# Moving the next head's scores, finishes and fetches to earlier steps of the head loop, and the reloads of sent outputs one granule later

## The chip, the cores and the metric

The program runs on one core of one Trainium2 chip. The metric is the device time of one execution in microseconds (us). Three runs of the kernel before gave 2140.3, 2144.18 and 2147.97 us; the median is 2144.18 us.

## The reference

One transformer block: RMSNorm, native sparse attention with three branches (compressed, selected, sliding window) over 512 tokens and 16 heads, an output projection, RMSNorm, a SwiGLU feed-forward network and a final RMSNorm. All eight selectable key blocks are taken, so the selected branch attends to all earlier tokens, as the window branch does.

```python
hn = rmsnorm(x, mix_norm_g)
q, kc, vc, ks, vs, kw, vw, gl = split(hn @ w_in)     # 16 query heads, 4 key/value groups
gates = sigmoid(gl)                                   # three per head
s_c = q @ compress(kc).T + bias_c ; s_s = q @ ks.T + bias ; s_w = q @ kw.T + bias
o = gates[0] * softmax(s_c) @ compress(vc) + gates[1] * softmax(s_s) @ vs + gates[2] * softmax(s_w) @ vw
h = x + o @ w_out
out = rmsnorm(h + swiglu(rmsnorm(h, ffn_norm_g)), final_norm_g)
```

## The kernel before, in words

Nothing is scheduled by a compiler: each engine executes its instructions in the order in which the Python code emits them, and an instruction that has to wait holds everything behind it on its engine or queue. So the order of the calls in the source is the order on each of TensorE (PE), VectorE (DVE), ScalarE (ACT), GpSimd (POOL) and on the DMA queue of SyncE (SP).

Products are done in three matmuls of a split into a high and a low part (`three`, lines 266 to 269). A weight granule of 128 x 1024 numbers is loaded into `raw`, and split by one ACT copy (`whi`, line 97) and one DVE subtraction (`wlo`, line 98). In the attention phase the granules are loaded through POOL's queue. `W.take` splits two granules ahead of the one that is used, so at every start of a granule one `whi` and one `wlo` are emitted.

**The head loop** (lines 875 to 902) runs over 16 heads with 12 steps each. A step consists of calls for the current head h, of calls for the next head h + 1, and of `pump`, which lets a generator `dense()` emit a piece of dense work on PE.

- `scores(h+1, t)` for the query tiles t = 3, 2, 1, 0: PE computes the scores of 128 queries (`s`, one PSUM tile for all), DVE adds the bias and takes the maximum in three operations (line 797), and ACT takes three exponentials into `p` (line 799).
- `finish(h+1, t)`: DVE normalizes and gates `p` (lines 804 to 811), transposes it in 32 x 32 blocks (line 812), and SP writes it to `d_p[t]` in DRAM in four DMAs (line 814).
- `fetch(t)`: SP reads `d_p[t]` back with partitions rearranged into its place of the tile `PT` (`ptr` in the profile, line 818). It has to wait for the four writes, and for the last reader of its place.
- `turn(h, b, kt)`, called nine times in steps 0 to 8: ACT copies a part of `PT` to a high part (`pth`, line 835), DVE makes the low part (`ptl`, line 839; the ninth, line 837, in place). The first two read only the place of t = 3, the next two t = 2 and 3, and so on; the seventh and eighth, and the ninth, read all four.
- `values`: PE multiplies a turned part with the values into the PSUM tile `o`, two steps after its turn; the last at step 11, followed by `head_out` (line 855), which copies `o` out by ACT, for heads below 12 to `d_o` in DRAM.
- `load_bias(h + 2)` at step 4: a bias tile by SP.

In the order before, step by step (t in brackets): 0 fetch(1), turn, finish(h, 0); 1 turn; 2 turn, scores(3); 3 fetch(0), turn, finish(3); 4 and 5 turn, at 5 scores(2); 6 turn, finish(2); 7 turn; 8 turn, fetch(3), fetch(2), scores(1); 9 finish(1); 11 scores(0), last values, head_out. Ahead of the loop the same calls are made for head 0 (lines 868 to 874).

**The dense work** comes in 13 units of 20800 (a made-up time, 32 yields of 650), and then 4 of 15600. `pump` lets exactly one unit pass per head until `at` = 13: a unit ends with step 8. A unit has four granules of 8 yields, so a granule starts, and a weight split is emitted, in the `pump` of steps 0, 3 and 6; the fourth granule splits the first of the next unit in its middle (line 275), in step 7. Units are `qpair` (queries of two later heads), `kpair` and `vpair` (keys and values of the next group). Their results are evacuated by pairs: for a query, DVE scales it (`yt`, line 319), ACT makes the high part (`qh`, line 292), DVE the low part (`ql`, line 293), in the pumps of steps 7 and 8. `drain_to(needed(h+1))` forces the unit that the next head needs, if it isn't done.

The last unit with h0 = 14 uses the normalized input `hn` for the last time. As soon as its granules are used, `reload_o(i)` brings the outputs of four finished heads from `d_o[i]` to `hn_l` through POOL's queue (1 MB each, line 695), and `split_o(k)` splits those of two heads between `hn_h` and `hn_l` (lines 699 and 700). Then `partial(cb)` multiplies heads 0 to 11 with `w_out`, with the remaining `split_o` calls in its first unit.

Of the kernel before, what the change touches and what calls it, by code (L numbers as in the profile page):

```python
# [19 lines left out]
S, D, H, DH, G, HPG = 512, 2048, 16, 128, 4, 4  # L20
# [153 lines left out]
def nsa_block(ctx: ExitStack, tc: tile.TileContext, x, rel_bias, mix_g, ffn_g, fin_g, w_in, w_out,  # L174
# [96 lines left out]
    def ws(ps, gi, g, c0=0, c1=S, start=None, end=None, of=None):  # L271

        for u in range(2):
            cs = slice(128 * u, 128 * (u + 1))
            if end and gi == 3 and u:
                W.ahead(3)
            for k in range(4):
                kk = 4 * gi + k
                st = (kk == 0) if start is None else (start and kk == 0)
                three(ps[u][:, c0:c1], g[0][:, k, cs], g[1][:, k, cs],  # L280
                      *(x[:, kk, c0:c1] for x in of or (hn_h, hn_l)), st, kk == KC - 1)
                if end and gi == 3 and k == 3:
                    end(u)
                yield 650
# [57 lines left out]
    def q_out(ps, h0):  # L342
        def end(u):
            Q[h0 + u] = tuple(qp.tile([128, S], F32R, name=f"q{n}") for n in "hl")
            split_from(normed(ps[u], SCALE), Q[h0 + u][0], Q[h0 + u][1])

        return end
# [282 lines left out]
    with ExitStack() as st2:  # L630
# [18 lines left out]
        def proj2():  # L649
            pool_ = (psx, ps2)[next(units) % 2]  # L650
            return [pool_.tile([128, 512], F32, name="proj") for _ in range(2)]

        def qpair(h0):
            ps = proj2()
            end = q_out(ps, h0)
            for i in range(4):
                yield from ws(ps, i, W.take(), end=end)
                if h0 == H - 2 and i < 3:
                    reload_o(i)
                if h0 == H - 2 and i > 1:  # L660
                    split_o(i - 2)
            done["n"] += 1
            yield None

# [29 lines left out]
        def reload_o(i):  # L694
            pool.dma_start(hn_l[:, 4 * i:4 * i + 4].bitcast(F32), d_o[i].rearrange("h p s -> p h s"))

        def split_o(k):
            h, l = (x[:, 2 * k:2 * k + 2] for x in (hn_h, hn_l))
            act(h, l.bitcast(F32), AF.Copy)  # L699
            dve.tensor_tensor(l, l.bitcast(F32), h.bitcast(F32), op=OP.subtract)  # L700
# [41 lines left out]
        def pump(h, step):  # L742
            at = h + (step + 4) / STEPS
            goal = 20800 * min(at, 13) + 22500 * max(at - 13, 0)
            while done["ns"] < goal:
                c = next(stream, "end")
                if c == "end":
                    return
                done["ns"] += c or 0
# [8 lines left out]
        def needed(h):  # L758

            return 4 * ((h - 2) // 4) + (1 if h % 4 > 1 else 3) if h > 1 else 0  # L760
# [4 lines left out]
        def load_bias(h):  # L765
            if h < H:
                TB[h] = ap_.tile([128, S], F32, name="tb")
                (nc.sync if h else pool).dma_start(TB[h], bass.AP(tensor=d_u.tensor, offset=d_u.offset + h * UL + 127,
                                                 ap=[[H * UL - 1, 128], [1, S]]))
# [5 lines left out]
        def scores(h, t):  # L775
            g, n = h // HPG, 128 * (t + 1)
            (qh, ql), (kh, kl) = Q[h], KK[g % 2]
            if t == NT - 1:
                HS[h] = dict(
                    mx=ap_.tile([128, NT, 3], F32, name="mx"), sm=ap_.tile([128, NT, 3], F32, name="sm"))  # L780
            s = HS[h]
            at = 224 + (512 if t == 1 else 0)
            cuts = [0, 288] + [c for c in (800, 1056) if c <= 32 + 2 * n]
            if cuts[-1] < 32 + 2 * n:
                cuts.append(32 + 2 * n)
            for c0, c1 in zip(cuts, cuts[1:]):
                three(sc[:, at + c0:at + c1], qh[:, tok(t)], ql[:, tok(t)], kh[:, c0:c1], kl[:, c0:c1], True, True)
            c = CX[t][:, :NCMP]
            regions = [(c, c, c, sc[:, at:at + NCMP], biasc[:, h, 24 - 8 * t:24 - 8 * t + NCMP])]
            bt = TB[h][:, S - n:].rearrange("p (n s) -> p n s", s=128)  # L790
            sw = sc[:, at + 32:at + 32 + 2 * n].rearrange("p (n b s) -> p b n s", b=2, s=128)
            for b in range(2):
                u = ap_.tile([128, S], F32, name="u")[:, :n]
                regions.append((u.rearrange("p (n s) -> p n s", s=128), u.rearrange("p (n j s) -> p j n s", j=4, s=32),
                                branch(t, b).rearrange("p j (n s) -> p j n s", s=32), sw[:, b], bt))
            for i, (u, v, p, ps, bias) in enumerate(regions):
                dve.tensor_tensor_reduce(out=u, in0=ps, in1=bias, op0=OP.add, op1=OP.min, scale=-1.0,
                                         scalar=1e38, accum_out=s["mx"][:, t, i:i + 1])
                act(p, v, AF.Exp, bias=s["mx"][:, t, i:i + 1], scale=-1.0, accum_out=s["sm"][:, t, i:i + 1])
            s[t] = [c] + [branch(t, b) for b in range(2)]  # L800

        def finish(h, t):
            r = HS[h]["sm"][:, t]
            dve.reciprocal(r, r)
            dve.tensor_mul(r, r, gates[:, t, h])
            for i, p in enumerate(HS[h].pop(t)):
                o = p
                if not i:
                    o = P[t][:, :3, runs[t] - 32:]
                    p = CX[t].unsqueeze(1).to_broadcast([128, 3, 32])  # L810
                dve.tensor_scalar(o, p, r[:, i:i + 1], None, op0=OP.mult)
            dve.transpose(P[t], P[t])
            for i in range(4):
                nc.sync.dma_start(d_p[t][:, :, i].rearrange("j a r -> a j r"), P[t][32 * i:32 * (i + 1)])

        def fetch(t):

            nc.sync.dma_start(PT[:, :, PT_STEP * t:PT_STEP * t + runs[t]], d_p[t].rearrange("j a i r -> (j a) i r"))
# [6 lines left out]
        def turn(h, b, kt):  # L825
            n = S - 128 * kt
            th = ap_.tile([128, 512], F32R, name="pth", bufs=3)
            tl = ap_.tile([128, 512], F32R, name="ptl") if b >= 0 else th
            rows = 128 if b >= 0 else 96
            if b < 0:  # L830
                src = arrived(rows, 64, 0, PT_STEP + 64)
            else:
                src = arrived(rows, PT_STEP * kt + 32 * (kt + 1) * b + 32 * kt, kt, PT_STEP + 32 * b)
            th4, tl4 = (x[:rows, :n].rearrange("p (t i s) -> p t i s", i=4, s=32) for x in (th, tl))
            act(th4, src, AF.Copy)  # L835
            if b < 0:
                dve.tensor_tensor(th4[32:64], src[32:64], th4[32:64].bitcast(F32), op=OP.subtract)
            else:
                dve.tensor_tensor(tl4, src, th4.bitcast(F32), op=OP.subtract)  # L839
            HS[h]["t", b, kt] = th[:rows, :n], tl[:rows, :n]  # L840
# [27 lines left out]
        for i in range(4):  # L868
            scores(0, 3 - i)
            if i > 1:  # L870
                fetch(5 - i)
            if i:
                finish(0, 4 - i)
            pump(-1, min(9 + i, 11.7))
        for h in range(H):
            seq = [(b, kt) for kt in (3, 2, 1, 0) for b in (0, 1)] + [(-1, 0)]
            for i in range(STEPS):
                if i == 4:
                    load_bias(h + 2)
                if i in (0, 3):  # L880
                    fetch(1 - i // 3)
                if i < 9:
                    turn(h, *seq[i])
                if i == 8 and h + 1 < H:
                    fetch(3)
                    fetch(2)
                if i == 0:
                    finish(h, 0)
                if h + 1 < H:
                    if i == 2:  # L890
                        drain_to(needed(h + 1))
                    if i % 3 == 2:
                        scores(h + 1, 3 - i // 3)
                    elif i % 3 == 0 and i:
                        finish(h + 1, 4 - i // 3)
                if 2 <= i < 10 or i == 11:
                    if i == 2 and h % HPG == 0:
                        drain_to(h)
                    values(h, *seq[min(i - 2, 8)])
                    if i == 11:  # L900
                        head_out(h)
                pump(h, i)
# [592 lines left out]
```

## Time and profile before

| What | Value |
|---|---|
| median of 3 runs | 2144.18 us |
| the profiled execution, its own time | 2143.05 us |
| its span, first to last instruction | 2141.3 us |
| around the span | 1.75 us |
| mean granted TensorE clock | 0.993 |
| busy: PEld / DVE / ACT / POOL | 1951.4 / 1634.8 / 929.2 / 128.0 us |
| head loop | about 222 to 713 us |

The profile's views have these columns. A timeline row is start, duration, engine, line, operation, written tile <- read tiles, shapes, and in brackets the idle time ahead of it with the one who ended it; "x2" joins two neighbours. A waits row is engine, written tile and line <- releaser: total us, times, longest. A window row is the stretch, then the busy time (and instructions) of PE, PEld, DVE, ACT, POOL, the granted clock, the DMA share, and GB/s. Ends of matmuls are modelled and overlap, so a PE that is busy for a whole stretch may still wait a little.

### The profile page before, as it was taken

To read this page: it belongs to the slowest core of one execution; us is meant where nothing else is said; L and a number is where in the kernel's file an instruction comes from. 1 tells how busy PE (TensorE), PEld (TensorE's weight loads), DVE (VectorE), ACT (ScalarE), POOL (GpSimd) and SP (SyncE) were. 2 spreads that over 40 slices of the span, in tenths; PEclk is the share of its full clock that TensorE was granted. 3 is DMA by queue.
4 is the path that set the end of the run, shared out by engine and by line. 5 is a ranking of instruction groups with operands and counts; after the bars stand their busy time and mean duration, and the time that the engine had idled before them with its cause. 6 is when DMAs were issued, how large, how long until landed. Compare 5 with 4: busy or idle time off the path is not lost.

```text
span 2141.3 us, 37148 instructions
## 1 busy us (share of the span) xinstructions
PE 2105.8 (98%) x14697; PEld 1951.4 (91%) x14697; DVE 1634.8 (76%) x2674; ACT 929.2 (43%) x1439; POOL 128.0 (6%) x209
## 2 busy tenths in 40 slices
PE   9999999999979999999999999999999999999998
PEld 7898788898969889899999999999999888989996
DVE  5565777877767347898888888888888787877785
ACT  5344455555544234434434344344344444544344
POOL 1000111111101000000000000000000000001000
PEclk9999999999989999999999999999999999999999
DMA  7554666666757633344434344343443776878894
GB/s 232 179 148 147 186 197 197 183 197 188 217 179 233 221 127 128 109 137 130 127 120 126 122 129 129 119 128 119 129 128 126 253 277 217 295 272 309 307 331 151
DMA packets 271867, 388.08 MB, mean 181 GB/s; under 512 B 34523, under 2 KB 204555, under 8 KB 271052
## 3 DMA queue, kind: packets, MB, share of 16 engines
q1 hardware_dynamic: 245932, 275.52, 41.0%
q0 software_dynamic: 23856, 105.98, 14.2%
q10 hardware_dynamic: 1904, 4.20, 0.5%
q8 instruction: 115, 1.88, 0.4%
q14 instruction: 60, 0.49, 0.1%
HBM read 320.52 MB, written 70.36 MB: 183 GB/s over the span
## 4 chain that ended last, share of the span: by engine, by line
PE 67%; DMA 1%; DVE 1%; ACT 1%; issue 0%; SPq 0%; ACTq 0%; DVEq 0%
PE f L268 19%; PE f L269 19%; PE f L267 19%; PE proj L267 1%; PE proj L268 1%; PE proj L269 1%; PE pp L267 1%; PE pp L268 1%; PE pp L269 1%; PE po L268 1%; PE po L267 1%; PE po L269 1%; DMA tt<-d_a 0%; PE pp L245 0%; DMA d_p<-p 0%
## 5 line engine op out<-in xcount | busy, mean ns | idle before, releaser
L98 DVE TENSOR_TENSOR wlo<-raw,whi 128x1024 fp32r<-128x1024 f32 (+1 forms) x226 | 270.7, 1200 | 115.2 <-ACT whi L97 115.1
L97 ACT ACTIVATE whi<-raw 128x1024 fp32r<-128x1024 f32 (+1 forms) x226 | 234.4, 1040 | 223.2 <-DVE raw L994 121.7
L994 DVE TENSOR_TENSOR tlo<-tt,thi 128x1536 fp32r<-128x1536 f32 (+2 forms) x135 | 197.1, 1460 | 109.7 <-ACT thi L1096 88.8
L267 PE MATMUL f<-hn_h,whi 128*128 128x256 f32 x984 | 271.7, 276 | 0.8 <-ACT E L1054 0.8
L269 PE MATMUL f<-hn_h,wlo 128*128 128x256 f32 x984 | 271.6, 276 | 0.0
L268 PE MATMUL f<-hn_l,whi 128*128 128x256 f32 x984 | 271.6, 276 | 0.0
L1091 ACT ACTIVATE whi<-raw 128x1024 fp32r<-128x1024 f32 x123 | 126.1, 1057 | 292.2 <-DVE raw L994 282.0
L267 PE MATMUL proj<-hn_h,whi 128*128 128x512 f32 x512 | 205.4, 401 | 0.5 <-ACT hn_h L402 0.5
L268 PE MATMUL proj<-hn_l,whi 128*128 128x512 f32 x512 | 201.7, 394 | 0.3 <-DVE hn_l L403 0.3
L269 PE MATMUL proj<-hn_h,wlo 128*128 128x512 f32 x512 | 201.6, 394 | 0.0
L267 PEld LDWEIGHTS f<-hn_h,whi 128*128 128x128 f32 x984 | 184.7, 188 | 1.2 <-ACT E L1054 1.2
L269 PEld LDWEIGHTS f<-hn_h,wlo 128*128 128x128 f32 x984 | 184.7, 188 | 0.0
L268 PEld LDWEIGHTS f<-hn_l,whi 128*128 128x128 f32 x984 | 184.7, 188 | 0.0
L1096 ACT ACTIVATE thi<-tt 128x1536 fp32r<-128x1536 f32 x82 | 121.9, 1487 | 84.1 <-PE f L268 84.1
L267 PE MATMUL proj<-whi,hn_h 128*128 128x256 f32 (+2 forms) x496 | 146.6, 296 | 5.9 <-ACT hn_h L699 5.9
L269 PE MATMUL proj<-whi,hn_l 128*128 128x256 f32 (+2 forms) x496 | 146.0, 294 | 2.1 <-DVE hn_l L700 2.1
L994 DVE TENSOR_TENSOR wlo<-raw,whi 128x1024 fp32r<-128x1024 f32 x123 | 147.0, 1223 | 0.0
L268 PE MATMUL proj<-wlo,hn_h 128*128 128x256 f32 (+2 forms) x496 | 145.5, 293 | 0.0
L269 PE MATMUL f<-whi,tlo 128*128 128x512 f32 x320 | 124.9, 390 | 0.6 <-DVE tlo L994 0.6
L268 PE MATMUL f<-wlo,thi 128*128 128x512 f32 x320 | 125.0, 391 | 0.3 <-DVE wlo L98 0.3
L267 PE MATMUL f<-whi,thi 128*128 128x512 f32 x320 | 124.7, 390 | 0.0
L839 DVE TENSOR_TENSOR ptl<-ptr,pth 128x128 fp32r<-128x128 f32 (+3 forms) x128 | 60.0, 485 | 76.7 <-ACT pth L835 72.9
(327 smaller groups left out, 6142.6 us busy)
## 6 DMA issues: line engine op xcount, KB each, us to landing
raw<-in_ffn_w_in SPq DMA_DIRECT2D x135, 512.0 KB, 3.6
raw<-in_ffn_w_out SPq DMA_DIRECT2D x88, 512.0 KB, 5.9
rawx<-in_ffn_w_in SPq DMA_DIRECT2D x41, 512.0 KB, 4.9
rawx<-d_a SPq DMA_DIRECT2D x31, 512.0 KB, 4.9
ah<-d_s POOLq DMA_DIRECT2D x16, 896.0 KB, 7.4
al<-d_s POOLq DMA_DIRECT2D x16, 896.0 KB, 10.1
raw<-in_nsa_w_in SPq DMA_DIRECT2D x24, 512.0 KB, 4.6
raw<-in_nsa_w_in POOLq DMA_DIRECT2D x24, 512.0 KB, 4.4
```

The source lines that it names most:

```text
L97: self.nc.scalar.activation(hi[:, :n], src, AF.Copy)
L98: self.nc.vector.tensor_tensor(lo[:, :n], src, hi[:, :n].bitcast(F32), op=OP.subtract)
L267: mm(o, ah, bh, start=start, stop=False, skip_group_check=True)
L268: mm(o, ah, bl, start=False, stop=False, skip_group_check=True)
L269: mm(o, al, bh, start=False, stop=stop, skip_group_check=True)
L839: dve.tensor_tensor(tl4, src, th4.bitcast(F32), op=OP.subtract)
L994: dve.tensor_tensor(o, a, b, op=OP.subtract)
L1091: act(h, r, AF.Copy)
L1096: act(h, ttf, AF.Copy)
```

## The change

The head loop's calls for the next head move to other steps. In the new order: 0 fetch(0), turn, scores(3); 1 turn, finish(3); 2 turn; 3 turn, scores(2); 4 turn, finish(2); 5 turn; 6 turn, scores(1); 7 turn, finish(1); 8 turn, fetch(3), fetch(2); 9 fetch(1), scores(0); 10 finish(0); 11 last values, head_out. `pump`, `turn`, `values` and `load_bias` stay in their steps. In numbers of steps, scores and finishes come two steps sooner, fetch(1) and fetch(0) three.

```diff
@@ qpair
             for i in range(4):
                 yield from ws(ps, i, W.take(), end=end)
-                if h0 == H - 2 and i < 3:
-                    reload_o(i)
-                if h0 == H - 2 and i > 1:
-                    split_o(i - 2)
+                if h0 == H - 2 and i:
+                    reload_o(i - 1)
+                    if i == 3:
+                        split_o(0)
+                        split_o(1)
@@ the head loop
+        fetch(1)
+        finish(0, 0)
         for h in range(H):
             seq = [(b, kt) for kt in (3, 2, 1, 0) for b in (0, 1)] + [(-1, 0)]
             for i in range(STEPS):
+                more = h + 1 < H
                 if i == 4:
                     load_bias(h + 2)
-                if i in (0, 3):
-                    fetch(1 - i // 3)
+                if i == 0:
+                    fetch(0)
                 if i < 9:
                     turn(h, *seq[i])
-                if i == 8 and h + 1 < H:
+                if i == 8 and more:
                     fetch(3)
                     fetch(2)
-                if i == 0:
-                    finish(h, 0)
-                if h + 1 < H:
-                    if i == 2:
+                if i == 9 and more:
+                    fetch(1)
+                if more:
+                    if i == 0:
                         drain_to(needed(h + 1))
-                    if i % 3 == 2:
+                    if i % 3 == 0:
                         scores(h + 1, 3 - i // 3)
-                    elif i % 3 == 0 and i:
-                        finish(h + 1, 4 - i // 3)
+                    elif i % 3 == 1:
+                        finish(h + 1, 3 - i // 3)
```

## The prediction

> **What bounds the kernel now.** I read the busy times first, then stretches of one head each, then who waits for whom, and last the timeline of one head.
>
> ```profile
> PE 2105.8 (98%) x14697; PEld 1951.4 (91%) x14697; DVE 1634.8 (76%) x2674; ACT 929.2 (43%) x1439; POOL 128.0 (6%) x209
> ...
> 283.58:313.46 29.88, 29.88 (x185) 26.72 (x184) 23.49 (x65) 15.12 (x41) 4.48 (x6) 1.00 0.69 198
> 523.16:553.05 29.89, 29.89 (x185) 26.71 (x184) 23.48 (x65) 15.24 (x43) 4.47 (x6) 1.00 0.69 200
> ```
>
> PE is busy for 98% of the span and for all of a head (two heads are shown, cut at their head_out), so whatever moves other work looks free, and at most some 35 us could be won. But the periods are equal to 0.02 us although the heads carry different dense units. Something with a fixed rhythm may set them. So I asked who waits in the undisturbed heads (240 to 585 us):
>
> ```profile
> DVE ptl L839 <- ACT pth L835: 48.5, 34, 2.2
> DVE ql L293 <- ACT qh L292: 8.6, 12, 0.7
> ...
> ACT cx L799 <- DVE mx L797: 112.0, 46, 3.7
> ...
> ACT pth L835 <- DMA ptr<-d_p: 1.2, 3, 0.6
> ```
>
> In the whole answers for DVE and ACT no row names PE: DVE waits for ACT alone, ACT for DVE and, for 1.2 us, for a fetch. The two hand work to each other in a closed loop, one head after the other. Here is one turn of it, ACT and then DVE:
>
> ```profile
> 523.64 0.30 ACT L835 ACTIVATE pth<-ptr 128x128 fp32r<-128x128 f32 x1
> ...
> 529.61 0.19 ACT L799 ACTIVATION_READ_ACCUMULATOR p<-u,mx 128x1 f32 x1
> ...
> 537.24 0.62 ACT L835 ACTIVATE pth<-ptr 128x512 fp32r<-128x512 f32 x1
> ...
> 543.86 1.05 ACT L97 ACTIVATE whi<-raw 128x1024 fp32r<-128x1024 f32 x1
> ...
> 548.40 0.19 ACT L799 ACTIVATION_READ_ACCUMULATOR p<-u,mx 128x1 f32 x1
> ...
> 553.52 0.30 ACT L835 ACTIVATE pth<-ptr 128x128 fp32r<-128x128 f32 x1
> ```
>
> ```profile
> 523.97 0.29 DVE L839 TENSOR_TENSOR ptl<-ptr,pth 128x128 fp32r<-128x128 f32 x1 [1.51 <-ACT pth L835]
> ...
> 525.80 1.18 DVE L98 TENSOR_TENSOR wlo<-raw,whi 128x1024 fp32r<-128x1024 f32 x1
> ...
> 527.43 0.18 DVE L797 CUSTOM_DVE_ANT_0 cx<-s,biasc 128x31 f32<-128x31 f32 x1
> ...
> 528.77 0.08 DVE L797 DVE_READ_ACCUMULATOR2_ANT mx<- 128x1 f32 x1
> 530.13 0.42 DVE L839 TENSOR_TENSOR ptl<-ptr,pth 128x256 fp32r<-128x256 f32 x1 [1.28 <-ACT pth L835]
> ...
> 535.32 0.18 DVE L797 CUSTOM_DVE_ANT_0 cx<-s,biasc 128x31 f32<-128x31 f32 x1
> ...
> 536.38 0.08 DVE L797 DVE_READ_ACCUMULATOR2_ANT mx<- 128x1 f32 x1
> 537.88 0.69 DVE L839 TENSOR_TENSOR ptl<-ptr,pth 128x512 fp32r<-128x512 f32 x1 [1.42 <-ACT pth L835]
> ...
> 543.99 0.69 DVE L293 TENSOR_TENSOR ql<-yt,qh 128x512 fp32r<-128x512 f32 x1 [0.70 <-ACT qh L292]
> 544.94 1.23 DVE L98 TENSOR_TENSOR wlo<-raw,whi 128x1024 fp32r<-128x1024 f32 x1 [0.26 <-ACT whi L97]
> 546.20 0.68 DVE L837 TENSOR_TENSOR pth<-ptr,pth 32x512 fp32r<-32x512 f32 x1
> 546.91 0.19 DVE L797 CUSTOM_DVE_ANT_0 cx<-s,biasc 128x31 f32<-128x31 f32 x1
> ...
> 547.71 0.08 DVE L797 DVE_READ_ACCUMULATOR2_ANT mx<- 128x1 f32 x1
> ...
> 549.14 0.69 DVE L293 TENSOR_TENSOR ql<-yt,qh 128x512 fp32r<-128x512 f32 x1 [0.74 <-ACT qh L292]
> 549.75 0.17 DVE L804 RECIPROCAL sm<-sm 128x3 f32<-128x3 f32 x1
> ...
> 551.76 0.15 DVE L797 CUSTOM_DVE_ANT_0 cx<-s,biasc 128x31 f32<-128x31 f32 x1
> ```
>
> From the first turn to the next head's is 553.52 - 523.64 = 29.88 us. DVE's idle brackets in it sum to 1.51 + 1.28 + 1.42 + 0.70 + 0.26 + 0.74 = 5.91 us; busy 23.5 and some joints make the rest. So the loop of DVE and ACT is full, and as slow as PE. **Two engines bound the heads together**, and a longer loop is paid in full, head by head.
>
> **The change, part by part.**
>
> **Scores against weight splits.** Instructions and bytes stay the same; only the order changes. Before, the step after scores begins with a turn and a finish, so ACT makes `whi` while DVE works on the finish, and `wlo` (525.80) needn't wait. Now scores(3), scores(2), scores(1) stand in steps 0, 3, 6, right ahead of the pump that emits a split. Behind the score operations the next thing on DVE is `wlo`; on ACT the exponentials come first, then `whi`, and 1.08 us after its start (543.86 to 544.94) `wlo`. What I get for DVE's idle time behind each:
>
> - scores(3): DVE is through 1.34 us after its start (527.43 to 528.77); ACT's last read starts at 2.18 (529.61), so `whi` at 2.27, `wlo` at 3.35: idle 2.01 where it was 1.28.
> - scores(2): DVE through at 1.06, ACT free at 1.92 (537.24), `wlo` at 3.00: idle 1.94 for 1.42.
> - scores(1): DVE through at 0.80, ACT free at 1.58 (548.40 + 0.09), `wlo` at 2.66: idle 1.86. Before, queries' evacuation lay there, with 0.74; that wait stays, in step 8, at the 0.70 of its twin.
> - scores(0): finish(0) now waits for the exponentials alone, by the same rows some 0.9 us, and the turn that waited 1.51 no longer does.
>
> The sum is 2.01 + 1.94 + 1.86 + 0.70 + 0.26 + 0.70 + 0.9 = 8.4 us, 2.5 more than 5.91. A `wlo` that follows a wait also holds DVE for 1.26 us (544.94 to 546.20) and not 1.10: three times, at most 0.5. So the loop alone takes 32.4 to 32.9, I say 32.6 us. Queued behind the waiting `wlo` are the next `ptl` and finish, and PE's values wait for `ptl`. PE's work doesn't grow, but it cannot run on: it already stands within two steps of the turns.
>
> **Fetch(3) loses its lead.** It goes out when turn(8) has left the tile, and the next head's first turn needs it.
>
> ```profile
> ptr<-d_p SPq DMA_DIRECT2D x16, 576.0 KB, 5.7
> ...
> 576.43 1.22 SPq L818 DMA_DIRECT2D ptr<-d_p  x2
> ```
>
> Before, the DVE part of turn(8) starts 22.56 us after the first turn (546.20), ends 0.68 later, and the fetch lands at about 22.56 + 0.68 + 5.7 = 28.9, 0.9 us ahead of need. In the new order finish(0) leaves the stretch ahead of turn(8) (1.6 of the 1.83 us from 523.97 to 525.80), scores(1) (0.80) and finish(1) (549.75 to 551.76, 2.01) enter it, and the idle time in it grows from 3.66 to 2.01 + 1.94 + 1.86 + 0.96 = 6.77. Turn(8) then starts at 22.56 - 1.6 + 2.8 + 3.1 = 26.9, with the slower restarts up to 27.3; the fetch lands at 27.1 + 0.7 + 5.7 = 33.5. That is later than the loop's own 32.6. So **the head takes 33.5 us**, 3.6 more. Behind this fetch on SP stand fetch(2), fetch(1), the writes of finish(0) and `d_o`; they have several steps left.
>
> The Trainium skill (DMA: Bandwidth & Descriptors, Anatomy of one DMA) gives 2.0 us plus bytes at 436 GB/s, fitted for GpSimd's path. By that this fetch would take an estimated 3.4 us and be hidden, and the second rival below would hold; the trace's 5.7 is used.
>
> **How many heads.** Heads 1 to 11 pay 3.6 each: 39.6. Head 0 starts from the same fetch and pays the excess over its own old course, about 1. Early dips of PE stay as they are.
>
> **Head 12, reloads and outputs.** Here the old order loses time:
>
> ```profile
> 589.22 0.53 SPq L818 DMA_DIRECT2D ptr<-d_p  x1
> ...
> 596.96 0.94 ACT L835 ACTIVATE pth<-ptr 128x384 fp32r<-128x384 f32 x2 [6.22 <-DMA ptr<-d_p]
> 597.54 0.69 PE L267 MATMUL o<-pth,v1h 128*128 128x384 f32 x1 [2.62 <-ACT pth L835]
> ...
> 604.37 0.63 ACT L835 ACTIVATE pth<-ptr 128x512 fp32r<-128x512 f32 x1 [3.90 <-DMA ptr<-d_p]
> ...
> 611.04 0.50 PE L268 MATMUL o<-ptl,v1h 128*128 128x512 f32 x1 [1.97 <-DVE ptl L839]
> ...
> 618.39 0.58 PE L267 MATMUL proj<-whi,hn_h 128*128 128x256 f32 x1 [5.91 <-ACT hn_h L699]
> ...
> 621.28 0.58 PE L269 MATMUL proj<-whi,hn_l 128*128 128x256 f32 x1 [2.10 <-DVE hn_l L700]
> ...
> 630.34 0.50 ACT L835 ACTIVATE pth<-ptr 128x128 fp32r<-128x128 f32 x2
> ```
>
> Fetch(1) and fetch(0) go out beside the reloads, and ACT waits 6.22 and 3.90 us for them. Three steps sooner they land ahead of need; these 10.1 us go. What is late next is `split_o`: PE's first partial product now needs split_o(0) too, since three splits stand in a row behind scores(0). From the first turn (553.52 + 29.88 = 583.4) to the next head's (630.34) head 12 takes 47.0 us. New: queries done at 29.9, scores and exponentials to 31.2, first split on DVE at 32.3, three of about 1.2 to 35.8, finish(0) 1.6, a fourth split, head_out 0.7, a `wlo` and the next split: 41. So 6 us are won, less than the waits removed. Reload_o(2) now goes out beside fetch(3) of head 13. A fetch beside a reload cost ACT up to 6.22 us here; but in this head some 13 us lie between the fetch (27.6) and the next first turn (41), so I take 0, with 6 as the other end. Reload_o(0) no longer waits on POOL for PE; the load behind it waits for `wlo` anyway: 0. `drain_to` two steps sooner finds its unit done since step 8: 0.
>
> **Heads 13 to 15.** Splits there fall on other steps and PE has more work per head; I take 0 (-2 to +4). In the last head fetch(0) comes in time:
>
> ```profile
> 705.00:720.00 15.00, 13.27 (x66) 10.12 (x65) 7.14 (x10) 5.87 (x8) 1.47 (x2) 1.00 0.66 209
> ```
>
> The 1.73 us that PE lacks in this stretch go.
>
> **Sum** against the profiled execution's own 2143.05 (span 2141.3 and 1.75 around it): 1 + 39.6 - 6 - 1.7 = 32.9, so 2176. The median of the runs shown is 1.1 above that execution; I leave that aside.
>
> **Rivals.**
>
> - *The fetch stays hidden*: it lands in 4.6 us or less, or turn(8) comes sooner. Then the loop's 32.6 counts: 2.7 x 11 - 6 - 1.7 = +22, **2165**. For it: in the undisturbed heads a fetch was late only three times, by 1.2 us in all. Against: 0.9 us of lead, and 4.5 are taken away. Chance 0.23; it also is what the skill's figure leads to.
> - *The fetch is slower*: fetch(1) and a weight load now share the time, and ACT's wait for a fetch that went out at 589.22 ended 7.7 us later. At 7.5 us a head takes 35.3: 5.4 x 12 - 7.7 = +57, **2200**. Chance 0.10.
> - *The loop isn't the bound* and the change does what it is named for. If, behind the scores, ACT and DVE have slack that the brackets don't show, a head stays at 29.9 us or less, and only the old stalls go: 2.62 + 1.97 of head 12, half of the 8.0 behind it, 1.7 at the end: -10, **2133**. For it: PE is 100% busy in the heads, and the fetches come earlier. Against: DVE's brackets name ACT at every place. It decides from the first full head on: its period is above or below 29.9. Chance 0.14.
> - *Nothing to see* (within 0.3%, which is about what a measurement of this kernel can tell from no change): gain and loss cancel at 1.2 us more per head. Chance 0.03.
>
> **How the numbers follow.** The forecast has 0.50. With the slower cases that makes slower 0.83, same 0.03, faster 0.14. The likeliest case alone spans 2168 to 2187 (heads 13 to 15, and 0.5 us per head either way). The range takes in the hidden fetch and part of the slow one, and leaves out the gain: 2154 to 2195.
>
> **What would show it.** Period from head_out to head_out near 33.5 us and PE busy near 29.7 of it; brackets of 1.8 to 2.0 us at L98 naming `whi`, three per head; ACT waiting for `ptr` by 1 to 2 us at each first turn; no long `ptr` wait in head 12; a burst of three L699 there with PE idle for some 9 us ahead of them. A period below 30 us would make the prediction wrong; one of 32.6 without `ptr` waits, its second step.

## The result and the profile after

Four runs of the changed kernel gave 2173.24 to 2176.09 us, median 2174.78 us. Four runs of the kernel before, taken beside them, had a median of 2144.3 us. The ratio is 1.0142, with a 95% interval of 1.0123 to 1.0162: the change makes the kernel **slower by 1.4%**. The profiled execution took 2174.97 us with a span of 2173.2 us, 31.9 us more than the span before, at a clock of 0.995 (0.993 before). In the new kernel the lines behind the first edit are numbered one higher: the turn is L836, L838 (ninth) and L840, the scores L798 and L800, the fetch L819, the reload L696, `split_o` L700 and L701.

The page's busy times, and then two heads cut from first turn to first turn (stretch, length, busy PE, PEld, DVE, ACT, POOL, clock, DMA share, GB/s):

```profile
PE 2110.7 (97%) x14697; PEld 1947.0 (90%) x14697; DVE 1640.6 (75%) x2674; ACT 932.0 (43%) x1439; POOL 129.9 (6%) x209
```

```profile
253.09:286.25 33.16, 30.33 (x145) 24.61 (x144) 24.16 (x65) 15.58 (x43) 4.47 (x6) 1.00 0.60 166
554.70:588.01 33.31, 29.98 (x172) 25.69 (x171) 23.85 (x65) 15.34 (x40) 4.78 (x6) 1.00 0.59 167
```

No engine has more work to do: DVE's busy time grew by 5.8 us over the whole span, PE's by 4.9. A head takes some 33 us instead of 29.9, and now PE lacks 3 us in each of them at full clock. The share of PE in the span hardly moved (98% to 97%), which would be easy to read over.

Who waits, from 260 to 600 us (waiting instruction <- releaser: total us, times, longest), on DVE and then on ACT:

```profile
DVE wlo L98 <- ACT whi L97: 60.3, 41, 1.9
DVE ptl L840 <- ACT pth L836: 10.4, 10, 2.0
DVE ql L293 <- ACT qh L292: 7.0, 10, 0.7
DVE sm L805 <- ACT p L800: 6.6, 8, 0.8
```

```profile
ACT pth L836 <- DMA ptr<-d_p: 19.7, 10, 2.7
```

DVE's main wait has changed its name. Before, it was `ptl` on `pth`, 48.5 us; now it is the low part of a weight on its high part. And ACT waits for a fetch in every head (10 times in these 340 us). The timeline of one head shows both, on DVE (the first turn, the three weight splits behind scores, and the ninth turn) and on SP and ACT:

```profile
520.35 0.29 DVE L840 TENSOR_TENSOR ptl<-ptr,pth 128x128 fp32r<-128x128 f32 x1 [1.00 <-ACT pth L836]
...
523.90 1.23 DVE L98 TENSOR_TENSOR wlo<-raw,whi 128x1024 fp32r<-128x1024 f32 x1 [1.93 <-ACT whi L97]
...
531.86 1.23 DVE L98 TENSOR_TENSOR wlo<-raw,whi 128x1024 fp32r<-128x1024 f32 x1 [1.85 <-ACT whi L97]
...
539.56 1.22 DVE L98 TENSOR_TENSOR wlo<-raw,whi 128x1024 fp32r<-128x1024 f32 x1 [1.77 <-ACT whi L97]
...
547.16 0.68 DVE L838 TENSOR_TENSOR pth<-ptr,pth 32x512 fp32r<-32x512 f32 x1
```

```profile
547.87 3.01 SPq L819 DMA_DIRECT2D ptr<-d_p  x3
```

```profile
520.01 0.31 ACT L836 ACTIVATE pth<-ptr 128x128 fp32r<-128x128 f32 x1 [1.92 <-DMA ptr<-d_p]
...
554.70 0.31 ACT L836 ACTIVATE pth<-ptr 128x128 fp32r<-128x128 f32 x1 [2.69 <-DMA ptr<-d_p]
```

Read in order of time, this is the closed loop of the new kernel. Three times DVE stands nearly 2 us ahead of a `wlo`. The ninth turn comes 27.15 us after the first (547.16 - 520.01), the fetches go out when it has ended, and ACT, which has had nothing else to do for 2.69 us, starts the next head's first turn 6.83 us after the first of them was issued. This head, with 34.69 us, is the longest of the eleven; they run from 32.71 to 34.69 us, with a mean of 33.42.

Head 12 has one long gap of PE. It ends when the first of a burst of four `split_o` on ACT is done:

```profile
651.96 3.88 ACT L700 ACTIVATE hn_h<-hn_l 128x1024 fp32r<-128x1024 f32 x4
```

```profile
653.05 0.58 PE L267 MATMUL proj<-whi,hn_h 128*128 128x256 f32 x1 [10.05 <-ACT hn_h L700]
```

To compare kernels, I cut each at the start of its ninth turns on DVE (the 32 x 512 subtraction), which can be found in all of them. The numbers are us of one profiled execution each:

| kernel | to the first ninth turn | per head, 11 heads | heads 12 and 13 | last two heads | rest of the span |
|---|---|---|---|---|---|
| before | 246.84 | 29.90 | 76.17 | 59.91 | 1429.5 |
| after | 246.72 | 33.44 | 73.67 | 56.05 | 1429.0 |
| difference | -0.1 | +3.54 (11 heads: +38.9) | -2.5 | -3.9 | -0.5 |

So all of the loss is in the eleven full heads, and 7.0 us of it are won back elsewhere.

### The profile page after: what moved, and what is told of

It is laid out like the page before. It is cut to its first block, busy times and chain, and to the rows that moved or that the text cites. A ratio compares the mean times of both kernels' runs of the same rounds, so it can differ in the third digit from the quotient of the medians.

```text
span 2173.2 us, 37131 instructions
## 1 busy us (share of the span) xinstructions
PE 2110.7 (97%) x14697; PEld 1947.0 (90%) x14697; DVE 1640.6 (75%) x2674; ACT 932.0 (43%) x1439; POOL 129.9 (6%) x209
## 4 chain that ended last, share of the span: by engine, by line
PE 78%; DVE 9%; ACT 4%; DMA 4%; issue 4%; SPq 0%; DVEq 0%; ACTq 0%
PE f L269 18%; PE f L268 18%; PE f L267 18%; PE proj L267 5%; PE proj L268 5%; PE proj L269 5%; DMA ptr<-d_p 3%; ACT whi L97 2%; DVE p L812 2%; DVE ptl L840 2%; DVE wlo L98 2%; ACT p L800 1%; DMA d_p<-p 1%; PE pp L269 1%; PE pp L268 1%
## 5 line engine op out<-in xcount | busy, mean ns | idle before, releaser
L269 PEld LDWEIGHTS proj<-hn_h,wlo 128*128 128x128 f32 x512 | 96.4, 188 | 21.6 <-DVE wlo L98 0.2
```

What stands on the lines that cost most here:

```text
L269: mm(o, al, bh, start=False, stop=stop, skip_group_check=True)
```

## Experiments

The theory is that of the prediction: DVE and ACT form a full loop; weight splits right behind scores lengthen it to some 32.6 us, and the fetch of t = 3, which can't leave before the ninth turn, lifts that to 33.4. Against it stood: that the sooner scores and finishes cost by themselves, that only the fetch or only the splits count, and that PE sets the pace. Four kernels undo or redo one part of this; the next three part the two halves of the change; the last four ask where the floor is.

**The dense work one step later.** The changed kernel, with `pump` shifted by one step, so that splits no longer stand right behind scores:

```diff
-            at = h + (step + 4) / STEPS
+            at = h + (step + 3) / STEPS
```

> The changed kernel with the pump's clock one step later, so that weight splits fall on steps 1, 4 and 7, where the finishes stand, and a unit ends in step 9. Theory (the splits stood right behind the scores, and DVE idled through exponentials and whi): each finish covers whi again, the idle time in front of wlo goes from some 1.9 us, three times per head, to 0, the loop of DVE and ACT falls to 29.6 to 30 us, turn(8) comes some 5 us sooner and the fetch is hidden. Head 12 keeps what the earlier fetches won. So 2133 to 2138 us, faster than both kernels. Rival (the earlier scores or the fetch alone make the head long): the head stays at 32 us or more, 2160 to 2175 us.

Measured: 2131.24 us (2130.69 to 2132.03, 5 runs), ratio to the kernel before 0.9938 (0.9924 to 0.9952). The heads take 29.63 us. This is **faster than both kernels**, with every call of the change at its new step. DVE's and ACT's waits (260 to 570 us):

```profile
DVE ptl L840 <- ACT pth L836: 41.4, 34, 1.3
...
DVE wlo L98 <- ACT whi L97: 3.0, 10, 0.5
```

```profile
ACT pth L836 <- DMA ptr<-d_p: 1.6, 4, 0.9
```

The waits of `wlo` fall to 3.0 us, and with them the fetch comes in time: the ninth turn is soon enough again. What made the changed kernel slow was where the splits stood, not the sooner scores.

**The fetch taken out of the loop.** The changed kernel, with the first turn of a head put behind the scores of t = 3 in its step, so that the fetch has some 2 us more:

```diff
-                if i < 9:
+                if i < 9 and (i or not more):
                     turn(h, *seq[i])
...
                         scores(h + 1, 3 - i // 3)
+                        if i == 0:
+                            turn(h, *seq[0])
```

> The changed kernel with turn(0) behind scores(3) within step 0, so that ACT has the exponentials to do while fetch(3) lands. Theory (fetch(3) is late by some 0.8 us of the loop, the splits cost the rest): the waits for ptr at the first turn shrink to near 0, the head takes 32.6 us instead of 33.4, and the time is 2165 us (2162 to 2169). Rival (the wait for the fetch is idle time of ACT that costs nothing): 2174 to 2176 us. Rival (the fetch alone is what costs): the head falls to 30 us, 2135 us.

Measured: 2160.98 us (2160.34 to 2163.14, 4 runs), ratio 1.0078 (1.0065 to 1.0092); 32.33 us per head. No wait of ACT for `ptr` is left in these heads, and the splits' wait stays (260 to 600 us):

```profile
DVE wlo L98 <- ACT whi L97: 49.3, 42, 1.9
```

So without the fetch the loop has 32.3 us, and the fetch adds 1.1. The edit also changes which calls are neighbours: DVE's waits for `whi` fall from 60.3 to 49.3 us, and in their place 12.0 us of waits of `ptl` for `pth` stand behind scores(3). The two nearly cancel. What is gone without a substitute are the 10.4 us that `ptl` waited in the changed kernel behind the late fetch, 1.0 per head, which agrees with the 1.1.

**The fetch made later.** The changed kernel with fetch(2) ahead of fetch(3):

```diff
                 if i == 8 and more:
-                    fetch(3)
                     fetch(2)
+                    fetch(3)
```

> The changed kernel with fetch(2) ahead of fetch(3) in step 8, which doubles the suspected cost: fetch(3) lands later by most of fetch(2)'s time. Theory (the landing of fetch(3) closes the loop): the head takes 1.5 to 2.5 us more, 35 to 36 us, the waits for ptr at the first turn grow by as much, and the time is 2192 to 2205 us. Rival (the fetch has slack): the head stays at 33.4 us, 2175 us.

Measured in one run: 2199.44 us, 35.25 us per head ((636.17 - 248.45) / 11, by the ninth turns), with the wait for the fetch grown from 19.7 to (260 to 600 us):

```profile
ACT pth L836 <- DMA ptr<-d_p: 34.9, 9, 4.6
```

Per wait that is 3.9 us instead of 2.0 (34.9 / 9 and 19.7 / 10), and each head is 1.8 us longer. In the changed kernel the fetch of t = 3 closes the loop.

**The same misplacement in the old order.** The kernel before, with `pump` two steps later, so that the splits stand right behind its scores:

```diff
-            at = h + (step + 4) / STEPS
+            at = h + (step + 2) / STEPS
```

> The kernel before, its scores, finishes and fetches where they were, with the pump's clock two steps later alone, so that its weight splits fall on steps 2, 5 and 8, right behind the scores. Theory (the place of the splits costs, not the early scores): DVE idles some 1.9 to 2.0 us in front of three wlo per head, the head takes 32.5 to 33.5 us instead of 29.9 with no wait for fetch(3), and the time is 2172 to 2185 us. Rival (the early scores themselves or the late fetch cost): the head stays at 30 us, 2140 to 2150 us.

Measured in one run: 2180.2 us and 33.04 us per head ((607.67 - 244.26) / 11).

```profile
DVE wlo L98 <- ACT whi L97: 60.4, 41, 1.9
```

The row is almost that of the changed kernel. Nothing of the change is in this kernel but the neighbourhood of scores and splits, and its heads lose nearly as much, 3.1 us instead of 3.5. Of the 35.4 us that it takes more than the kernel before (2144.83 beside it), 34.5 are what its eleven heads have lost.

**The reloads alone.** The kernel before with only the edit of `qpair`:

```diff
-                if h0 == H - 2 and i < 3:
-                    reload_o(i)
-                if h0 == H - 2 and i > 1:
-                    split_o(i - 2)
+                if h0 == H - 2 and i:
+                    reload_o(i - 1)
+                    if i == 3:
+                        split_o(0)
+                        split_o(1)
```

> The kernel before with only the second part of the change: reloads one granule later, the first two split_o together. Theory: the head loop is untouched, so the heads keep 29.9 us, and in head 12 the fetches of t = 1 and 0 still go out beside reloads, so ACT still waits some 6 and some 4 us for them; the reloads are late by one granule, so PE's wait for the first split (5.9 us before) grows by a few us. 2143 to 2150 us, ratio 1.000 to 1.003. Rival (the later reloads, not the sooner fetches, took the two waits out of head 12): the waits for the fetches shrink below 2 us each, 2134 to 2139 us.

Measured: 2135.55 us (2135.43 to 2136.74, 4 runs), ratio 0.9961 (0.9948 to 0.9975). **My theory fell here, and the rival held**: the two fetch waits of head 12 are gone, and its PE gap for the first split stays at 6.23 us (5.91 before). The SP and POOL queues show why. Before (SP, then POOL):

```profile
580.32 3.69 SPq L814 DMA_DIRECT2D d_p<-p  x4
584.05 0.44 SPq L860 DMA_DIRECT2D d_o<-stage  x1
589.22 0.53 SPq L818 DMA_DIRECT2D ptr<-d_p  x1
```

```profile
580.20 0.75 POOL L695 DMA_DIRECT2D hn_l<-d_o  x1 [3.35 <-PE proj L268]
```

With the reloads one granule later:

```profile
580.06 2.49 SPq L815 DMA_DIRECT2D d_p<-p  x4
583.21 0.34 SPq L861 DMA_DIRECT2D d_o<-stage  x1
584.90 0.53 SPq L819 DMA_DIRECT2D ptr<-d_p  x1
...
589.21 0.52 SPq L819 DMA_DIRECT2D ptr<-d_p  x1
```

```profile
587.57 0.76 POOL L696 DMA_DIRECT2D hn_l<-d_o  x1
```

The first reload used to start together with the four writes of `d_p[1]`. The fetch has to wait for these writes, and it went out at 589.22 instead of 584.90: 4.3 us were lost ahead of the fetch. The issues from 578 to 600 us (size, and the median us from issue to landing), before and with the later reloads:

```profile
d_p<-p SPq DMA_DIRECT2D x4, 80.0 KB, 7.7
ptr<-d_p SPq DMA_DIRECT2D x1, 320.0 KB, 7.6
```

```profile
d_p<-p SPq DMA_DIRECT2D x4, 80.0 KB, 3.9
ptr<-d_p SPq DMA_DIRECT2D x1, 320.0 KB, 3.5
```

The first row of each pair are the writes that the fetch waits for; beside the reload they take twice as long. The second row is the fetch itself. It too took twice as long before: when it went out, the second reload was on its way (issued at 587.83). So about half of the delay arose ahead of the fetch and half in it. I had looked at what runs beside the fetch and not at what runs beside the writes that it waits for.

**The old reloads in the new loop.** The kernel after with the `qpair` of before (the diff above, reversed).

> The kernel after with the reloads and splits of the kernel before. Theory: the heads stay at 33.4 us, the gain of head 12 comes from the sooner fetches and stays; the first split is ready sooner, so PE's gap of 10 us in head 12 gets shorter, but only by what the split was late for its reload and not for its place behind the scores: 2168 to 2177 us. Rival (the later reloads made the gain in head 12): the waits for the fetches come back, head 12 takes 47 us again, 2178 to 2183 us.

Measured: 2176.34 us (2174.42 to 2177.95, 4 runs), ratio 1.015 (1.0134 to 1.0165), which can't be told from the changed kernel. Heads 12 and 13 take 73.42 us (73.67 there); the longest wait for a fetch in head 12 behind its first turn is 1.8 us. So in the new loop the sooner fetches alone remove head 12's waits, in the old one the later reloads alone do: **the two halves of the change remove the same 10 us of waits, and that can be done once.** Nor do the later reloads make PE's gap: it is 9.1 us against 10.0.

**The faster version with the old reloads.** The first experiment's kernel with the `qpair` of before.

> The version with the pump shifted by one step, with the reloads and splits of the kernel before. Heads at 29.8 us as there. If the reloads one granule later cost PE some of its wait for the first split, 2127 to 2130 us; if they keep a fetch of head 12 undisturbed, 2132 to 2136 us. Theory leans to the first, since the fetches are three steps sooner in any case.

Measured: 2131.96 us (2130.69 to 2132.2, 5 runs), ratio 0.9942 (0.9929 to 0.9954), the same as with the later reloads. The lower outcome, to which the theory leaned, didn't come: the old reloads win nothing over the later ones here either, as in the new loop of the kernel after.

**The dense work one step ahead.** The changed kernel, with `pump` shifted the other way:

```diff
-            at = h + (step + 4) / STEPS
+            at = h + (step + 5) / STEPS
```

The first sentence of the expectation names the direction wrongly: by this number the dense work runs one step ahead of where the change has it, with splits in steps 11, 2, 5 and 6.

> The kernel after with its dense work one more step behind than in the version that ran with the pump shifted by one: weight splits in steps 11, 2, 5 and 8 or thereabouts. Theory: no split stands right behind scores, so DVE's waits of 1.9 us at the low part of the weights are gone; what is left is the fetch of t = 3, which goes out behind the ninth turn and is as late as that turn is. The evacuation of queries stands ahead of the ninth turn then, so the fetch may be late by 1 to 2 us: 30.0 to 31.5 us per head, 2130 to 2150 us. Rival (scores that come sooner cost by themselves, wherever the splits are): 32.5 us per head or more, over 2160 us.

Measured in one run: 2132.26 us, 29.72 us per head ((578.23 - 251.28) / 11), a little less than the 30.0 to 31.5 expected. `wlo` waits 3.0 us in all (260 to 570 us) and ACT waits for the fetch a little, as expected:

```profile
ACT pth L836 <- DMA ptr<-d_p: 15.6, 10, 2.0
```

The heads are as short as in the first experiment in spite of 1.5 us of such waits in each. With the splits elsewhere, on either side, the sooner scores cost nothing.

**Who sets the period.** PE is busy for a whole head of the kernel before, so one instruction of DVE was issued twice per head, the low part of the seventh turn:

```diff
-                dve.tensor_tensor(tl4, src, th4.bitcast(F32), op=OP.subtract)
+                for _ in range(2 if b == 0 and kt == 0 else 1):
+                    dve.tensor_tensor(tl4, src, th4.bitcast(F32), op=OP.subtract)
```

> The kernel before with one instruction of VectorE issued twice in each head, the low part of the seventh turn (128 x 512, 0.69 us, 0.61 us between neighbours). Theory (the loop of VectorE and ScalarE is full and sets the period, PE only keeps up): the period of the heads, from one ninth turn to the next, grows from 29.90 us by the whole 0.6 us, to 30.5; the time by some 7 to 9 us. Rival (PE, busy for all of a head, sets the period, and the two others have slack that their waits don't show): the period stays at 29.9 and the time within 2 us of before.

> The same doubled instruction in the version with the pump shifted by one step. If VectorE and ScalarE still set the period there: 29.63 us from ninth turn to ninth turn becomes 30.2, and the time 2138 to 2141 us. If PE is the bound there by now: below 29.8 us, 2130 to 2133 us. I lean to the first with 6 in 10, because VectorE's waits in a head have about the same sum as before.

Measured in one run each: 2157.06 us and 30.67 us per head in the kernel before (29.90 without), 2140.89 us and 30.33 us in the first experiment's (29.63 without). The pair in the first of them:

```profile
545.84 1.42 DVE L840 TENSOR_TENSOR ptl<-ptr,pth 128x512 fp32r<-128x512 f32 x2 [1.42 <-ACT pth L835]
```

One such instruction takes 0.69, so the second adds 0.73, and the periods grow by 0.77 and 0.70. DVE's time is paid in full, although DVE is busy for under 80% of a head. So PE alone doesn't set the period. How far below the loop PE's own time lies, this test can't tell; the next one does, for the faster version. The kernel before lost 12.8 us where 7 to 9 were expected: 8.5 are those of its eleven heads (0.77 each), and the rest is spread over the stretches around them (1.6 in heads 12 and 13, 2.2 in the last two by the ninth turns).

**A shorter loop.** The first experiment's kernel with the finish ahead of the turn in steps 1, 4 and 7:

```diff
+                if more and i in (1, 4, 7):
+                    finish(h + 1, 3 - i // 3)
                 if i < 9:
                     turn(h, *seq[i])
...
-                    elif i % 3 == 1:
-                        finish(h + 1, 3 - i // 3)
+                    elif i == 10:
+                        finish(h + 1, 0)
```

> The version with the pump shifted by one step, and in steps 1, 4 and 7 the finish stands ahead of the turn. Theory (the loop of VectorE and ScalarE still sets the period): behind the scores VectorE waits there for the turn's high part, which stands on ScalarE behind three exponentials, some 1.3 us three times a head; the finish needs the exponentials alone, so that it waits 0.8 us, and the high part is made meanwhile. 0.4 to 0.5 us are won three times a head: a period of 28.3 to 28.9 us if PE can go as fast, and 2117 to 2124 us. Rival (PE with 29.7 us busy in a head is a floor that lies close below): the period stays above 29.4 us and the time at 2129 to 2132 us, and PE's waits stay near zero.

Measured: 2130.58 us (2129.49 to 2132.86, 6 runs), ratio 0.994 (0.9927 to 0.9953), the same as without the edit, and 29.57 us per head. The waits of `ptl` for `pth`, 41.4 us in the first experiment's kernel, nearly vanish, shorter ones of the finish for its exponentials take their place as planned, and new names appear among DVE's waits (260 to 560 us):

```profile
DVE sm L805 <- ACT p L800: 29.5, 33, 1.0
...
DVE cx L798 <- PE s L269: 2.5, 9, 0.3
DVE ptl L840 <- PE o L268: 1.5, 8, 0.2
```

```profile
391.37:421.06 29.69, 29.69 (x146) 25.13 (x146) 23.74 (x65) 15.52 (x42) 5.95 (x8) 1.00 0.73 195
510.25:539.93 29.68, 29.68 (x146) 25.12 (x145) 23.74 (x65) 15.52 (x42) 5.95 (x8) 1.00 0.71 195
```

For the first time DVE waits for PE in nearly every head, a little each time, and PE waits for nobody. The rival held. From the third period on, the heads take 29.66 to 29.84 us, no less than in the first experiment's kernel (29.53 to 29.89): PE's own time, some 29.7 us, is within about 0.1 us of the loop there, so making the loop shorter wins nothing.

## Why the prediction was right

The time, 2174.78 us, is 1.2 us from the 2176 on record. By its own steps:

- **Two engines bound the heads together, and a longer loop is paid in full**: right, and shown by the doubled instruction (+0.77 us per head for 0.73 us). That PE was 100% busy in the windows proved nothing; that no wait of DVE or ACT named PE pointed the right way. The other sign, periods equal to 0.02 us, was weaker than it read: it holds for the two heads shown, and of the eleven periods from head_out to head_out eight lie between 29.87 and 29.90 us, the others at 29.80, 29.81 and 30.48.
- **Splits behind scores, 2.01, 1.94 and 1.86 us**: measured 1.93, 1.85 and 1.77. The loop was put at 32.6; with the fetch taken out it has 32.3, and the old order with its splits behind its scores has 33.0.
- **Fetch(3) loses its lead**: the ninth turn was put 26.9 to 27.3 us behind the first and came after 27.15; the head was put at 33.5, and the first turns (253.09 to 620.72, eleven periods) are 33.42 us apart. The later fetch moved the period one for one.
- **Heads 1 to 11**: 39.6 predicted, 38.5 measured ((620.72 - 253.09) - (583.34 - 254.16)).
- **Head 0**: predicted +1, measured -1.1 (the first turn of head 1 at 253.09 instead of 254.16). The step failed in sign: the ninth turn of head 0 comes at the same time in both kernels (246.72 and 246.84), 25.1 us after the first turn and not some 27 as in a full head. The fetch behind it landed early enough for the next first turn to come sooner than in the old order, and what I charged as an excess wasn't there.
- **Head 12**: 47.0 before, 41 predicted, 42.9 measured (620.72 to 663.61), so 4.1 us won and not 6. The sequence held: no long wait for a fetch, a burst of `split_o`, and PE idle for 10.05 us ahead of its first product from it, where 9 was said. Up to the third split it held to 0.1 us (first split on DVE at 32.31 us for 32.3, third over at 35.81 for 35.8). What the row of the prediction lacked is a wait ahead of head_out, which it put at 0.7 us right behind the fourth split. ACT stood for 5.38 us, and DVE behind it for 2.61, until PE had finished the last values in `o`:

```profile
661.22 0.60 ACT L292 ACTIVATE hn_h<-o 128x512 fp32r<-128x512 f32 x1 [5.38 <-PE o L851]
```

```profile
661.85 0.69 DVE L293 TENSOR_TENSOR hn_l<-o,hn_h 128x512 fp32r<-128x512 f32 x1 [2.61 <-ACT hn_h L292]
```

PE came out of its gap at 653.05 and ran at a granted clock of 0.50 and 0.54 (650 to 655 and 655 to 660 us). DVE's wait of 2.61 us is more than the 1.9 by which the term was too good.
- **Reload_o at 0**: in the new loop it is (2176.34 and 2174.78 can't be told apart). The reason given for head 12's old waits, fetches beside reloads, was half of it: the first reload also delayed the writes that the fetch waits for. In the old loop this half of the change is worth 8.7 us (2144.24 to 2135.55), so a zero that is right in one order was not a zero in the other.
- **Heads 13 to 15 and the end**: head 13 +2.4 (33.49 instead of 31.10), head 14 -0.2, and from the first turn of the last head to the end of the span -3.5, where 0 and -1.7 stood. In sum -1.3 against -1.7, from terms that were each off by about 2.

The terms add up to 38.5 - 1.1 - 4.1 - 1.3 = 32.0; the spans differ by 31.9. The errors of head 0, of head 12 and of the full heads partly cancel.

Of the rivals, the hidden fetch (the first of the list, though the sentence on the skill's figure calls it the second) is what the second experiment built, at 2160.98 us for a price of 2165. The page of the Trainium skill behind it (DMA: Bandwidth & Descriptors, Anatomy of one DMA) led to an estimated 3.4 us for that fetch. The trace disagrees: in the head shown above, 6.83 us passed from the issue to the turn that waited for it, and the measurement decides. The rival in which the change does what it is named for came true in another kernel: with the splits moved away, all of it is faster than before.

## What to carry to other kernels

Where two in-order engines hand work to each other, their order is a resource: moving one call next to another that ends on the partner engine can cost more than any of the moved work, though nothing is added. Before moving a call, list what will stand right behind it on both engines, and after it move the neighbours too; one number (`+ 4` to `+ 3`) turned a loss of 1.4% into a gain of 0.6%. To learn whether a loop of other engines bounds a stretch in which one engine is always busy, issue one instruction of that loop twice: if the period grows by all of it, it does. That doesn't mean that the busy engine has slack: in the faster version the period grew by 0.70 of 0.73 us, although PE's own time was within 0.1 us of it. How much there is to win shows only when the loop is made shorter and a wait for the busy engine appears.

## What was unexpected in the hardware

A short gap of PE can cost again after it. In head 12 of the kernel before, PE has no matmul for 2.6 us, up to 597.54 us (windows of 2.5 us, the clock behind POOL's column):

```profile
595.00:597.50 2.50, 0.00 (x0) 0.00 (x0) 0.00 (x0) 0.54 (x2) 1.06 (x2) 0.92 0.79 241
597.50:600.00 2.50, 2.46 (x6) 1.97 (x7) 2.09 (x8) 1.65 (x6) 0.00 (x0) 0.50 0.95 264
600.00:602.50 2.50, 2.50 (x7) 1.93 (x7) 0.00 (x0) 0.48 (x2) 0.00 (x0) 0.50 0.99 325
602.50:605.00 2.50, 2.50 (x11) 2.19 (x10) 0.00 (x0) 0.63 (x2) 0.00 (x0) 0.71 0.85 304
605.00:607.50 2.50, 2.50 (x15) 2.23 (x14) 2.36 (x7) 2.42 (x4) 0.00 (x0) 1.00 0.04 14
```

The timeline of PE has the same shape in both stretches:

```profile
600.22 0.63 PE L267 MATMUL proj<-hn_h,whi 128*128 128x512 f32 x1
600.65 0.63 PE L268 MATMUL proj<-hn_l,whi 128*128 128x512 f32 x1
...
604.77 0.39 PE L268 MATMUL proj<-hn_l,whi 128*128 128x512 f32 x1
604.99 0.39 PE L269 MATMUL proj<-hn_h,wlo 128*128 128x512 f32 x1
```

When the matmuls come back, the granted clock is 0.50 for 5 us, and one follows the other at 0.43 us (600.65 - 600.22) instead of 0.22; "busy" says 2.50 of 2.50 in both. In the kernel with only the reloads moved there is no gap here, and the clock is 1.00 from 580 to 600 us.

The length of the gap alone doesn't decide this. In the kernel before, a gap of 1.97 us that ended at 611.04 left the clock at 1.00 for the 1.4 us until PE stopped again; in the first experiment's kernel a gap of 2.13 us that ended at 222.29 was followed by 0.50. In the old order with the splits behind its scores, six gaps of 2.54 to 2.60 us stand in the heads. Behind two of them (ended at 257.16 and 587.54) the clock stays at 1.00 for the next 7 us; behind the other four (323.62, 389.04, 455.41, 520.83) it is 0.50 for about 3 us, twice only from 0.5 to 1 us after the matmuls came back. What decides between them, these runs don't show.
